# Layer 0's modulation products on four column quarters, the first norm's steps in the planned list, and new lists for both layers

## The chip, the cores and the metric

The kernel runs on one core of a Trainium2 chip. The metric is the device time of one execution in microseconds (us); before the change the median of three runs is 1832.78 us (1830.01 to 1833.64).

## What is computed

Two layers of a diffusion backbone over 512 latent tokens and 256 context tokens of width 1024, all in 32-bit floats. What matters here is the head of each layer: a conditioning vector `c` (and a second one, `c_ctx`, for the context tokens) goes through silu and is multiplied by a 1024 x 6144 matrix. The 6144 results are six vectors of 1024, which shift and scale the normalised tokens and gate the two sub-layers.

```python
mod = silu(c) @ w_mod[layer] + b_mod[layer]           # 6 vectors of 1024, for the latent tokens
mod_c = silu(c_ctx) @ w_mod[layer] + b_mod[layer]     # the same for the context tokens
sh1, sc1, g1, sh2, sc2, g2 = split(mod, 6)
h = rmsnorm(x, norm_g[0]) * (1 + sc1) + sh1           # 512 tokens; the context likewise
qa, ka, va, qr, kr, vr, gr, z, xbc, dt = split(h @ w_in[layer])
# attention, retention and a state-space group, concatenated, @ w_out, gated by g1;
# then a squared-ReLU MLP on rmsnorm(x) * (1 + sc2) + sh2, gated by g2
```

## The kernel before, in words

The 6144 columns of `w_mod` are cut into twelve sections of 512 (two for each of the six vectors). Sections 0 and 1 are the shift and 2 and 3 the scale of the first norm, 4 and 5 the first gate, 6 to 9 shift and scale of the second norm. A section is a sum over eight K-blocks of 128 rows. Layer 0's sections 0 to 9 are computed in four ways. `mod_exact` (sections 0, 2 and 3, line 370) multiplies the two-column `csil` (both conditioning vectors) in full float by one 128 x 512 block at a time, into two rows of PSUM; each product leaves two matmul records. `mod_sums` (section 1, lines 417 to 425) accumulates on VectorE and sums over the partitions with sixteen short matmul records. `mod_split` (sections 4 and 5, line 396) rounds the weights to a high part (ScalarE, line 277) and a low part (GpSimd, line 278) and multiplies both by a four-column stationary block. `mod_whole` (sections 6 to 9, line 381) is `mod_exact` with 512 KB loads of two K-blocks. `mod_cols` then turns the rows of a section into columns with four transposes (`mps`, line 208) and adds the bias.

`start` is the prologue: it loads the six token tiles (`x`), takes their norms, issues sections 0 to 3, transposes the tiles between the products (`xps`), and when all products are issued it calls `modulate` (lines 499 to 505), which scales and shifts each tile and splits it into a high part `h_h` and a low part `h_l`. One call of `modulate` is half a tile; there are twelve.

After that each layer is a set of named units (`kv0`, `xa3.`, `as20`, `md7`, ...), which are issued in the order of the written list `PLAN[layer]`. The names that matter: `kvN` the key/value projection of tile N (`kvp`, lines 523 to 525), `xwN`, `xaN`, `xbN` the state-space projection (`xbc`), `as`, `at`, `ao` scores, transposes and outputs of the attention by head, `rp`, `rs`, `rd`, `rt`, `ro`, `rn`, `ur` the steps of a retention head, `mdN` the N-th step of sections 4 to 9, a step being two K-blocks, and `woN` the first products of the output projection. The order of emission sets priorities; instructions of different units may still be exchanged on an engine by the framework's scheduler. On each engine and on the load queue of SyncE the result is one fixed order, in which an instruction that waits holds back all behind it. In layer 1 `KV_LATE` units `kv` are held behind the last matmul of layer 0's MLP.

Of the kernel before, what the change touches and what calls it, by code (L numbers as in the profile page):

```python
# [42 lines left out]
def shape_constants():  # L43
# [26 lines left out]
    KV_LATE=1,  # L70
# [5 lines left out]
    MOD="GGGVGG",  # L76
# [4 lines left out]
    CUT="443444",  # L81
)
PLAN = {
    0: """
        kv0 kv1 xw3 kv2 xa3. kv3 kv4 kv5 xa3 xb3 kp1 xw5 xa5. xa4. xa4 xc3 xb4 xc4 xt3 xa5 xb5 xc5 de xw0 kp0
        xt4 xa0. xa0 xa1. ds xb0 dr xa1 xb1 xc0 xw2 xa6. xa6 xb6 xa2. xc1 xc6 xa2 xt0 xt1 xb2 xc2 xt2 qa0. qa0
        g0 f10 f11 m1 qa1. qa1 qa2. sv00 sv01 sd01 f00 g1 f01 qa2 m0 sk b0 qa3. qa3 sd00 f20 f21 b1 sv10 si10
        qa4. qa4 sv11 si11 m2 sd11 qa5. f30 sd10 f31 qa5 sv20 m3 si20 si21 b2 zz0. sd20 sv21 sv30 zz0 sd21
        sv31 f40 f41 si30 m4 sd30 zz1. zz1 si31 zz2. zz2 sd31 f50 f51 sv41 b3 zz3. m5 zz3 si41 sd41 sv40 b4
        si40 sd40 zz4. zz4 zz5. zz5 b5 si50 si51 sg0 sg1 sg4 sg5 sg2 sg3 sn aqs rc ak0 aq0 aq1 as00 at00 as01  # L90
        at01 kr0. av as10 kr0 as02 ao00 at02 as03 at03 as04 as05 at04 at05 ao02 ao01 aq2 kr1. kr1 at10 as11
        as12 at11 kr2. kr2 ao10 kr3. kr3 at12 as13 at13 kr4. kr4 as14 kr5. ak1 ao11 aq3 as20 at20 as21 kr5
        at21 ao20 qg0. qg0 at14 as15 at15 as22 at22 as23 as24 at23 ao21 ao12 at24 as25 qg1. qg1 at25 ao22 qg2.
        qg2 aq4 as30 at30 as31 at31 ao30 qg3. qg3 as32 at32 as33 as34 at34 at33 ao31 as35 qg4. qg4 at35 ao32
        qg5. qg5 aq5 as40 at40 as41 md0 at41 ao40 as42 as43 as44 rw0 at44 at42 at43 as45 at45 ao41 md1 ao42
        as50 at50 as51 at51 md2 rl0 md3 ao50 as52 at52 as53 at53 rw1 md4 as54 at54 mx as55 rv ao51 md5 rp0
        at55 rx0 rx1 rl1 rs0 rp1 md6 rd0 md7 md8 ao52 md9 us2 md10 md11 rt0 md12 md13 md14 rd1 md15 rg0 ro00
        us0 md16 md17 md18 md19 md20 us1 ro01 ro02 md21 md22 rn0 rx2 rw2 md23 rg1 rt1 rs1 rl2 rp2 ro10 md24
        ro11 ro12 rn1 ur0 rw3 rl3 rs2 rd2 ua0 rp3 rx3 ua1 rt2 ro20 ro21 ro22 ua2 wp rg2 wo0 rs3 rn2 rd3 rg3
        rt3 wo1 wo2 wo3 ro30 wo4 wo5 ro31 ro32 rn3 wq wo6 wo7 wo8 ur1  # L100
    """.split(),
    1: """
        kv0 kv1 kv2 kv3 kv4 kv5 km0 km1 xw3 xa3. xa3 xb3 xa4. xa4 xb4 xc3 xt3 xw5 xa6. xa5. xc4 kp1 xa5 xt4 de
        xc5 xa6 kp0 xc6 xw0 xa1. ds dr xa0. xa0 xa1 xb0 xb1 xc0 xt0 xc1 xt1 xw2 xa2. xa2 xb2 xc2 xt2 qa0. g0
        f00 f10 qa0 f01 g1 m0 f11 sv00 qa1. sd00 sk qa1 m1 sv01 sd01 f20 qa2. qa2 b0 f21 sv11 sv10 b1 qa3.
        sd11 sd10 m2 zz0. f30 zz0 sv20 qa3 b2 si21 f31 m3 zz1. zz1 si20 sd20 zz2. sv21 si30 zz2 sd21 zz3. zz3
        sv30 f40 sd30 si31 aqs b3 sv31 f41 sv40 rc si40 sd31 f50 si41 sd40 m4 f51 m5 sv41 si50 sd41 b4 si51 b5
        sg0 sg3 kr0. sg1 sg2 sn aq0 av ak0 aq1 as00 at00 as01 at01 ao00 kr0 as02 at02 kr1. as03 at03 aq2 ao01
        kr1 kr2. kr2 as10 as11 at10 as12 at12 as13 at11 ao10 at13 aq3 as20 ak1 as21 at20 ao11 kr3. as22 at21
        kr3 kr4. kr4 ao20 at22 as23 at23 kr5. ao21 aq4 as30 at30 as31 as32 at31 kr5 qg0. ao30 as33 qg0 at32  # L110
        at33 ao31 qg1. qg1 aq5 as40 at40 as41 qg2. qg2 at41 as42 ao40 as50 at42 as43 qg3. at43 rw0 ao41 rv
        as51 as52 qg3 at50 at51 mx ao50 at52 as53 at53 ao51 rl0 rx0 rp0 rx1 ua0 rw1 rl1 rd0 rp1 rg1 us0 us1
        rs0 rd1 rg0 rt0 ro00 ro01 rn0 rw2 rl2 rp2 rx2 rs1 rt1 ro10 rs2 ro11 rn1 rx3 us2 ur0 rd2 rw3 rl3 rp3
        rt2 wp rd3 rg2 ro20 rs3 ro21 rn2 wo0 ua1 wo1 rg3 wo2 rt3 ro30 wo3 wo4 ua2 ro31 wo5 rn3 ur1 wq wo6 wo7
        wo8
# [18 lines left out]
def tile_hybrid_backbone(  # L134
# [166 lines left out]
    chl = cp.tile([128, KC, 4], F32R, name="chl")  # L301
    V.tensor_copy(chl[:, :, 0:4:2], csil)
    V.tensor_tensor(chl[:, :, 1:4:2], csil, chl[:, :, 0:4:2].bitcast(F32), ALU.subtract)
# [23 lines left out]
    def mod_cols(l, sec, q, nrow):  # L327
# [3 lines left out]
        if q.shape[0] == 128:  # L331
# [9 lines left out]
        if nrow == 2:  # L341
            V.tensor_tensor(tk, o, bcol, ALU.add)
        else:
            u = sm.tile([128, 4, 4], F32, tag="mc_u", name=f"mu{l}_{sec}")
            S.activation(u, o, AF.Copy)
            V.tensor_tensor(tk, u[:, :, 0:4:2], u[:, :, 1:4:2], ALU.add)
            V.tensor_tensor(tk, tk, bcol, ALU.add)
# [16 lines left out]

    def mod_exact(l, sec, raw, row):
        q = pB([2, 512], f"mq{l}_{sec}")
        for k in range(KC):
            v = raw(f"m{l}_{sec}_{k}")
            nc.sync.dma_start(v, w_mod[l, k * 128 : (k + 1) * 128, sec * 512 : (sec + 1) * 512])
            T.matmul(q, csil[:, k, :], v, start=k == 0, stop=k == KC - 1)  # L370
            yield
        r = row([2, 512], f"mr{l}_{sec}")
        S.activation(r, q, AF.Copy)
        mod_cols(l, sec, r, 2)

    def mod_whole(l, sec, row):
        q = pB([2, 512], f"mq{l}_{sec}")
        for u in range(4):
            r = wraw(wcols(w_mod[l], 0, [(sec * 512, 0, 512)])(2 * u, 2), (128, 2, 512), f"m{l}_{sec}_{u}")
            for k in range(2):  # L380
                T.matmul(q, csil[:, 2 * u + k, :], r[:, k], start=u + k == 0, stop=u + k == 4)
            if u == 3:
                r = row([2, 512], f"mr{l}_{sec}")
                S.activation(r, q, AF.Copy)
            yield
        mod_cols(l, sec, r, 2)

    def mod_split(l, sec, row):
        q = pB([4, 512], f"mq{l}_{sec}")
        for u in range(4):  # L390
            if u % 2 == 0:
                hu, lu = wunit(wcols(w_mod[l], 2 * u, [(sec * 512, 0, 512)]), (128, 4, 512), f"m{l}_{sec}_{u}", eng(KNOBS["MOD"][sec - 4]))
            h, lo = hu[:, 2 * (u % 2) : 2 * (u % 2) + 2], lu[:, 2 * (u % 2) : 2 * (u % 2) + 2]
            for k in range(2):
                for w in (h, lo):
                    T.matmul(q, chl[:, 2 * u + k, :], w[:, k, :], start=(u == 0 and k == 0 and w is h),
                             stop=(u == 3 and k == 1 and w is lo))
            if u == 3:
                r = row([4, 512], f"mr{l}_{sec}")
                S.activation(r, q, AF.Copy)  # L400
            yield
        mod_cols(l, sec, r, 4)
# [154 lines left out]
    def mixers(l, mp, hT, alloc_mix, kvw=None):  # L557
# [9 lines left out]
        par = pars[l]  # L567
# [92 lines left out]
        kv_gen = tm_group("kv", 268, [(KA, 0, 256), (DT0, 256, 12)], 6, c_kv, (pB, pC), kvw[:1])  # L660
# [7 lines left out]
        for t in range(6):  # L668
            unit(f"kv{t}", lambda t=t: kv_step(t), f"kv{t - 1}" if t else None)
# [145 lines left out]
        def conv_w(js):  # L815
            h, lo = kvw[1] if js[0] == 3 and len(kvw) > 1 else xbc_unit(l, js, eng(KNOBS["X_LO"][4 * l + {3: 0, 5: 1, 0: 2, 2: 3}[js[0]]]))
# [3 lines left out]
        for js in ((3, 4), (5, 6), (0, 1), (2,)):  # L820
            unit(f"xw{js[0]}", lambda js=js: conv_w(js))
            for j in js:
                first = {}
                unit(f"xa{j}.", lambda j=j, first=first: next(first.setdefault("g", conv_in(j, 0))), f"xw{js[0]}")
                unit(f"xa{j}", lambda first=first: next(first["g"], 0), f"xa{j}.")
                if wc or j < 5:
                    unit(f"xb{j}", lambda j=j: run(conv_in(j, 1)), f"xa{j}")
# [157 lines left out]
        for nm, n, cols, nt, consume in (("qa", 384, [(QA, 0, 384)], NQ, c_qa), ("zz", 384, [(Z0, 0, 384)], NQ, c_z),  # L985
                                         ("kr", 512, [(KR, 0, 512)], 6, c_krv), ("qg", 512, [(QR, 0, 256), (GR, 256, 256)], NQ, c_qg)):
            gen = tm_group(nm, n, cols, nt, consume, split=True)
            for t in range(nt):
                unit(f"{nm}{t}.", steps(gen), f"{nm}{t - 1}" if t else None)
                unit(f"{nm}{t}", steps(gen), f"{nm}{t}.")  # L990
# [170 lines left out]
        unit("rc", ret_const)  # L1161
# [406 lines left out]
    def start(mp, hT):  # L1568
# [3 lines left out]
        acc = mp.tile([128, 1536], F32, tag="m6", name="acc_m", bufs=KNOBS["M6"])[:, :1024].rearrange("p (s n) -> p s n", s=2)  # L1572

        def weave(a, b):
            for _ in a:
                next(b, None)
                yield
            yield from b

        row = lambda shape, name: mp.tile([128, 512], F32, tag="fcol", name=name)[: shape[0]]  # L1580

        def gens():
            yield from mod_exact(0, 0, raws[0], row)
            yield from weave(mod_exact(0, 2, raws[0], row), mod_sums(0, 1, acc, raws[1]))
            yield from mod_exact(0, 3, raws[1], row)

        gemv = gens()
# [92 lines left out]
```

## Time and profile before

| | |
|---|---|
| median of the runs | 1832.78 us |
| the profiled execution, whole | 1831.16 us |
| its span, first to last instruction | 1829.4 us |
| TensorE busy | 1737.7 us (95%) |
| VectorE busy | 1208.8 us (66%) |
| ScalarE busy | 701.7 us (38%) |
| mean granted TensorE clock | 0.979 |

Busy time of TensorE is read with care: matmuls are pipelined, so that a record is longer than the distance to the next one. Where costs are added up, the distance from start to start counts. The two stretches that the change touches most are the first 46 us, up to the first key/value product, and the stretch from 340 to 440 us, which holds the end of layer 0's attention, its retention heads and sections 4 to 9.

### The profile page before, as it was taken

To read this page: it belongs to the slowest core of one execution; us is meant where nothing else is said; L and a number is where in the kernel's file an instruction comes from. 1 tells how busy PE (TensorE), PEld (TensorE's weight loads), DVE (VectorE), ACT (ScalarE), POOL (GpSimd) and SP (SyncE) were. 2 spreads that over 40 slices of the span, in tenths; PEclk is the share of its full clock that TensorE was granted. 3 is DMA by queue.
4 is the path that set the end of the run, shared out by engine and by line. 5 is a ranking of instruction groups with operands and counts; after the bars stand their busy time and mean duration, and the time that the engine had idled before them with its cause. 6 is when DMAs were issued, how large, how long until landed. Compare 5 with 4: busy or idle time off the path is not lost. (4 is left out here: it accounts for less than half of the span.)

```text
span 1829.4 us, 24602 instructions
## 1 busy us (share of the span) xinstructions
PE 1737.7 (95%) x8991; PEld 1433.7 (78%) x8991; DVE 1208.8 (66%) x2474; ACT 701.7 (38%) x1270; POOL 342.4 (19%) x376
## 2 busy tenths in 40 slices
PE   7998999998999999999999999999988999999997
PEld 2887978657777888888888878887877788888886
DVE  5788976767567566566566587898877644444445
ACT  5553366743561201211201266545762622222222
POOL 0127222312000100100100111453121111111112
PEclk9999999998999999999999999999987999999999
DMA  8420443476435434444344443233343523333332
GB/s 282 123 61 30 133 123 101 119 204 177 162 120 137 126 105 126 128 113 117 116 116 116 128 150 116 68 106 104 106 121 85 179 67 94 102 94 100 104 95 92
DMA packets 189077, 217.00 MB, mean 119 GB/s; under 512 B 67666, under 2 KB 142236, under 8 KB 188956
## 3 DMA queue, kind: packets, MB, share of 16 engines
q1 hardware_dynamic: 188956, 215.43, 39.7%
q8 instruction: 71, 1.16, 0.3%
q14 instruction: 50, 0.41, 0.1%
HBM read 189.66 MB, written 25.72 MB: 118 GB/s over the span
## 5 line engine op out<-in xcount | busy, mean ns | idle before, releaser
L523 PE MATMUL f<-h_h,wh_f 128*128 128x512 f32 (+1 forms) x800 | 281.2, 352 | 1.4 <-ACT h_h L504 1.4
L524 PE MATMUL f<-h_l,wh_f 128*128 128x512 f32 (+1 forms) x800 | 281.7, 352 | 0.8 <-DVE h_l L505 0.8
L525 PE MATMUL f<-h_h,wl_f 128*128 128x512 f32 (+1 forms) x800 | 282.3, 353 | 0.0
L523 PE MATMUL f<-wh_g,uh 128*128 128x512 f32 x640 | 252.8, 396 | 4.6 <-DVE acc L1532 1.9
L524 PE MATMUL f<-wl_g,uh 128*128 128x512 f32 x640 | 252.5, 394 | 0.0
L525 PE MATMUL f<-wh_g,ul 128*128 128x512 f32 x640 | 251.8, 393 | 0.0
L1504 POOL TENSOR_TENSOR r<-r 128x768 f32<-128x768 f32 (+1 forms) x64 | 94.0, 1469 | 834.2 <-ACT r L1503 823.1
L277 ACT ACTIVATE wh_f<-wr_f 128x1024 fp32r<-128x1024 f32 x64 | 66.4, 1054 | 375.2 <-PE f L525 135.4
L1534 DVE TENSOR_TENSOR acc<-acc,f 128x512 f32<-128x512 f32 x140 | 96.1, 687 | 120.8 <-PE f L525 119.4
L523 PEld LDWEIGHTS f<-h_h,wh_f 128*128 128x128 f32 x800 | 153.2, 192 | 23.4 <-ACT h_h L504 1.5
L524 PEld LDWEIGHTS f<-h_l,wh_f 128*128 128x128 f32 x800 | 152.2, 190 | 23.0 <-DVE h_l L505 1.0
L525 PEld LDWEIGHTS f<-h_h,wl_f 128*128 128x128 f32 x800 | 152.4, 191 | 20.9
L461 DVE SCALAR_TENSOR_TENSOR ga<-wr_mg,cg_a,ga 128x512 f32<-128x512 f32 x216 | 153.7, 764 | 15.2 <-DMA wr_mg<-in_w_mod_dram 15.1
L523 PEld LDWEIGHTS f<-wh_g,uh 128*128 128x128 f32 x640 | 120.1, 188 | 33.9 <-DVE acc L1532 2.3
L525 PEld LDWEIGHTS f<-wh_g,ul 128*128 128x128 f32 x640 | 120.2, 188 | 28.6
L524 PEld LDWEIGHTS f<-wl_g,uh 128*128 128x128 f32 x640 | 120.3, 188 | 27.3
L1503 ACT ACTIVATE r<-f 128x768 f32<-128x768 f32 (+1 forms) x64 | 44.7, 698 | 192.2 <-PE f L525 128.2
L1505 DVE CAST uh<-r 128x768 fp32r<-128x768 f32 (+1 forms) x64 | 32.3, 505 | 123.7 <-POOL r L1504 123.7
L278 DVE TENSOR_TENSOR wl_g<-wr_g,wh_g 128x1024 fp32r<-128x1024 f32 x62 | 76.7, 1242 | 53.8 <-ACT wh_g L277 53.8
L278 DVE TENSOR_TENSOR wl_f<-wr_f,wh_f 128x1024 fp32r<-128x1024 f32 x64 | 77.7, 1221 | 50.1 <-ACT wh_f L277 50.1
L277 ACT ACTIVATE wh_g<-wr_g 128x1024 fp32r<-128x1024 f32 x64 | 67.3, 1056 | 96.6 <-DMA wr_g<-in_w_ff_dram 55.2
L523 PE MATMUL xbc<-h_h,wh_xbc 128*128 128x512 f32 (+1 forms) x208 | 71.9, 345 | 1.9 <-ACT cin L785 1.9
(403 smaller groups left out, 3711.0 us busy)
## 6 DMA issues: line engine op xcount, KB each, us to landing
wr_f<-in_w_ff_dram SPq DMA_DIRECT2D x64, 512.0 KB, 3.8
wr_g<-in_w_ff_dram SPq DMA_DIRECT2D x64, 512.0 KB, 3.6
wr_mg<-in_w_mod_dram SPq DMA_DIRECT2D x192, 128.0 KB, 2.9
wr_m<-in_w_mod_dram SPq DMA_DIRECT2D x24, 512.0 KB, 4.0
m<-in_w_mod_dram SPq DMA_DIRECT2D x32, 256.0 KB, 5.1
wr_o<-in_w_out_dram SPq DMA_DIRECT2D x16, 512.0 KB, 4.2
wr_xbc<-in_w_in_dram SPq DMA_DIRECT2D x14, 512.0 KB, 5.4
xmid<-xt SPq DMA_DIRECT2D x10, 512.0 KB
```

The lines of the kernel that those rows point to most:

```text
L277: S.activation(hv[:, a0 : a0 + an], r, AF.Copy)
L278: (lo_eng or V).tensor_tensor(lv[:, a0 : a0 + an], r, hv[:, a0 : a0 + an].bitcast(F32), ALU.subtract)
L461: V.scalar_tensor_tensor(acc[:, s], r2[:, k % 2], w, acc[:, s], ALU.mult, ALU.add)
L523: T.matmul(o, a[0], b[0], start=first, stop=False)
L524: T.matmul(o, a[0], b[1], start=False, stop=False)
L525: return T.matmul(o, a[1], b[0], start=False, stop=last)
L1503: S.activation(r, q[:, :NT], AF.Relu)
L1504: G.tensor_tensor(r, r, r, ALU.mult)
L1505: V.tensor_copy(uh, r)
L1534: V.tensor_tensor(acc[tt][:, ns], acc[tt][:, ns], qs[tt][half], ALU.add)
```

## The change

The products of layer 0's ten sections all take one form. The stationary block is `cwide[:, k, :]`, `csil` widened from 2 to 32 columns with zeros, and K-block k goes to rows 32j to 32j+31 of a 128 x 512 PSUM tile, j = k mod 4. Each quarter thus sums two K-blocks. The four transposes of `mod_cols` become four products of the 128 x 512 copy with `qsum`, a 128 x 2 matrix that adds the four quarters and turns rows into columns at once. `mod_split` is gone, with its conversions, and section 1 no longer uses VectorE.

The prologue is cut into units (`xl` load, `xq` square, `xr` root, `xs` scale, `xu` transpose, `xm` modulate by half tile, `mo` one K-block of sections 0 to 3, `kw`, `pc`, `pr` loads of weights and parameters), and `kv` into halves of four K-blocks; these stand in the list with the rest. Both lists are written anew, and `KV_LATE` goes from 1 to 4.

```diff
-    chl = cp.tile([128, KC, 4], F32R, name="chl")
+    cwide = cp.tile([128, KC, 32], F32, name="cwide")
+    G.memset(cwide, 0.0)
+    G.tensor_copy(cwide[:, :, 0:2], csil)
+    qsum = cp.tile([128, 2], F32, name="qsum")
+    V.tensor_reduce(qsum, ident.rearrange("p (j r) -> p r j", r=32)[:, 0:2, :], AX.X, ALU.add)
...
             for k in range(4):
-                transpose(o[:, k, :], q[:, k * 128 : (k + 1) * 128])
+                T.matmul(o[:, k, :], q[:, k * 128 : (k + 1) * 128], qsum, start=True, stop=True)
...
+    def mod_quarter(q, k, v):
+        j = k % 4
+        T.matmul(q[32 * j : 32 * j + 32], cwide[:, k, :], v, start=k < 4, stop=k >= KC - 4)
...
     def mod_exact(l, sec, raw, row):
-        q = pB([2, 512], f"mq{l}_{sec}")
+        q = pB([128, 512], f"mq{l}_{sec}")
...
-            T.matmul(q, csil[:, k, :], v, start=k == 0, stop=k == KC - 1)
+            mod_quarter(q, k, v)
...
-                yield from (mod_whole if sec >= 6 else mod_split)(0, sec, row)
+                yield from mod_whole(0, sec, row)
...
-    KV_LATE=1,
+    KV_LATE=4,
...
 PLAN = {
     0: """
-        kv0 kv1 xw3 kv2 xa3. kv3 kv4 kv5 xa3 xb3 kp1 xw5 xa5. xa4. xa4 xc3 xb4 xc4 xt3 xa5 xb5 xc5 de xw0 kp0
...
+        xl0 xl2 xl3 xl4 xl5 xq0 xl1 xq4 xq3 xq1 xq2 xq5 xr0 xs3 mo00 xs0 xs4 mo01 mo02 xs2 pc mo03 xs5 mo04
+        mo05 mo06 xs1 mo10 mo20 mo21 mo22 xu2 mo07 xu3 xu1 xu0 mo08 mo23 mo11 mo12 mo13 xu5 mo24 mo14 mo25
+        mo15 mo26 mo27 mo16 mo17 mo28 mo18 kw xm02 mo30 mo31 xu4 mo32 mo33 mo34 mo35 mo36 mo37 mo38 xm10 xm11
+        xm01 xm00 xm03 xm12 xm05 xm15 pr kv0. xm13 kv0 kv1. xm04 kv1 kv2. kv2 xw3 xa3. kv3. xm14 kv3 kv4. kv4
...
-        us0 md16 md17 md18 md19 md20 us1 ro01 ro02 md21 md22 rn0 rx2 rw2 md23 rg1 rt1 rs1 rl2 rp2 ro10 md24
+        md7 md8 ao52 rd0 md9 us2 md10 md11 rt0 md12 md13 rg0 md14 rd1 md15 ro00 us0 md16 md17 rx2 md18 md19
```

## Rows read from the trace of the kernel before

**Rows 1.** The page's first part: busy us, share of the span, instructions.
```profile
PE 1737.7 (95%) x8991; PEld 1433.7 (78%) x8991; DVE 1208.8 (66%) x2474; ACT 701.7 (38%) x1270; POOL 342.4 (19%) x376
```
**Rows 2.** Windows of the prologue: busy us of engines, clock, DMA share, GB/s.
```profile
core 0: us, PE busy (x) PEld busy (x) DVE busy (x) ACT busy (x) POOL busy (x), PEclk, DMA share, GB/s
10.00:20.00 10.00, 6.81 (x12) 1.15 (x13) 2.05 (x13) 7.26 (x10) 0.00 (x0) 1.00 0.86 285
30.00:40.00 10.00, 10.00 (x55) 5.33 (x55) 8.90 (x18) 4.37 (x9) 0.00 (x0) 1.00 1.05 331
50.00:60.00 10.00, 9.87 (x78) 9.54 (x77) 7.99 (x21) 10.00 (x23) 0.00 (x0) 1.00 0.30 97
```
**Rows 3.** Timeline of TensorE in the prologue: start, us, operation, count [idle before].
```profile
13.19 3.57 PE L370 MATMUL mq<-m,csil 128*2 128x512 f32 x4 [9.60 <-DMA m<-in_w_mod_dram]
26.48 1.88 PE L370 MATMUL mq<-m,csil 128*2 128x512 f32 x4
28.29 1.10 PE L208 MATMUL xps<-ident,x 128*128 128x128 f32 x8
29.31 1.02 PE L370 MATMUL mq<-m,csil 128*2 128x512 f32 x2
36.73 1.84 PE L425 MATMUL mq<-sel,acc_m 128*128 128x1 f32 x16
38.50 7.03 PE L370 MATMUL mq<-m,csil 128*2 128x512 f32 x16
48.55 0.41 PE L208 MATMUL mps<-ident,mr 2*128 2x2 f32 x4 [1.96 <-ACT mr L373]
```
**Rows 4.** Timeline of the load queue: the last three weight loads of section 3.
```profile
36.56 0.33 SPq L369 DMA_DIRECT2D m<-in_w_mod_dram  x1
...
39.55 0.33 SPq L369 DMA_DIRECT2D m<-in_w_mod_dram  x1
...
40.41 0.33 SPq L369 DMA_DIRECT2D m<-in_w_mod_dram  x1
```
**Rows 5.** All products of the sections, by line: min/median/max ns, first and last start.
```profile
L381 PE MATMUL mq<-wr_m,csil x64: 591/592/593, 356.7 to 418.0; 128*2 128x512 f32 x64
L396 PE MATMUL mq<-wh_m,chl x16: 387/396/397, 341.9 to 360.1; 128*4 128x512 f32 x16
L396 PE MATMUL mq<-wl_m,chl x16: 387/394/472, 342.1 to 360.3; 128*4 128x512 f32 x16
L277 ACT ACTIVATE wh_m<-wr_m x8: 1042/1060/1081, 284.0 to 354.2; 128x1024 fp32r<-128x1024 f32 x8
L278 POOL TENSOR_TENSOR wl_m<-wr_m,wh_m x8: 2374/2392/2706, 285.1 to 355.3; 128x1024 fp32r<-128x1024 f32 x8
```
**Rows 6.** Timeline of TensorE in the stretch of sections 4 to 9.
```profile
341.85 0.39 PE L396 MATMUL mq<-wh_m,chl 128*4 128x512 f32 x1
342.08 0.39 PE L396 MATMUL mq<-wl_m,chl 128*4 128x512 f32 x1
...
370.08 1.02 PE L381 MATMUL mq<-wr_m,csil 128*2 128x512 f32 x2
...
394.07 0.41 PE L208 MATMUL mps<-ident,mr 4*128 4x4 f32 x4
394.40 1.88 PE L381 MATMUL mq<-wr_m,csil 128*2 128x512 f32 x4
...
413.25 5.31 PE L381 MATMUL mq<-wr_m,csil 128*2 128x512 f32 x12
```
**Rows 7.** Windows of that stretch, and of the half clock in it.
```profile
340.00:380.00 40.00, 38.18 (x204) 21.98 (x202) 30.19 (x65) 30.95 (x63) 15.62 (x8) 1.00 0.65 177
380.00:440.00 60.00, 54.02 (x275) 33.37 (x276) 38.80 (x113) 17.01 (x32) 8.94 (x11) 0.89 0.77 215
...
420.00:440.00 20.00, 15.51 (x87) 14.70 (x87) 14.10 (x37) 6.32 (x11) 6.61 (x7) 0.66 0.83 213
```
**Rows 8.** TensorE's longest wait in that stretch, in the timeline.
```profile
432.53 1.51 PE L208 MATMUL sT<-ident,ry 128*128 128x128 f32 x6 [3.27 <-DVE ry L1269]
```
**Rows 9.** TensorE's two waits where layer 1 begins, in the timeline.
```profile
1094.21 1.09 PE L208 MATMUL nps<-ident,tt 128*128 128x128 f32 x8 [3.88 <-ACT tt L510]
...
1103.73 0.39 PE L525 MATMUL kvp<-wh_kv,h_l 128*128 128x268 f32 x1 [1.91 <-POOL h_l L505]
```

More of the change, by code (lines that the diff above doesn't have):

```diff
@@ L81 @@
     CUT="443444",
+    SECS="EEEE",
+    RAW="0101",
 )
@@ L90 @@
[L90 to L94, printed above, removed]
@@ L116 @@
+        wo5 rn3 ur1 wq wo6 wo7 wo8
     """.split(),
@@ L330, in mod_cols @@
         k0 = 4 * (sec % 2)
-        if q.shape[0] == 128:
+        if len(q.shape) == 3:
             o = q
@@ L386, in mod_whole @@
         mod_cols(l, sec, r, 2)
[L388 to L402, printed above, removed]
     def mod_sums(l, sec, acc, raw=None):
@@ L1566, in load_par, with start @@
             nc.sync.dma_start(pars[l][:, o : o + n], ap.partition_broadcast(128))
[L1568 removed]
+    def start(mp, hT, kvw, unit):
         raws = [lambda name, tag=tag, n=n: mp.tile([128, 776], F32, tag=tag, name=name, bufs=n)[:, :512]
                 for tag, n in (("u3", 6), ("t3", KNOBS["T3"]))]
[L1572 to L1578, printed above, removed]
[L1580 to L1591 removed]
@@ new lines, in start, with mod_step @@
+        row = lambda shape, name: mp.tile([128, 512], F32, tag="fcol", name=name)[: shape[0]]
+        gens = {}
+        def mod_step(sec):
+            if sec not in gens:
+                raw = raws[int(KNOBS["RAW"][sec])]
+                if KNOBS["SECS"][sec] == "S":
+                    acc = mp.tile([128, 1536], F32, tag="m6", name=f"acc_m{sec}", bufs=KNOBS["M6"])[:, :1024]
+                    gens[sec] = mod_sums(0, sec, acc.rearrange("p (s n) -> p s n", s=2), raw)
+                else:
+                    gens[sec] = mod_exact(0, sec, raw, row)
+            return next(gens[sec], 0)
@@ new lines, in mod_end @@
+        def mod_end(sec):
+            while mod_step(sec) != 0:
+                pass
+        unit("pc", lambda: load_pcol(0))
+        unit("pr", lambda: load_par(0))
+        unit("kw", lambda: kvw.append(kv_unit(0)))
+        for sec in range(4):
+            for k in range(KC):
+                unit(f"mo{sec}{k}", lambda sec=sec: mod_step(sec), f"mo{sec}{k - 1}" if k else None)
+            unit(f"mo{sec}8", lambda sec=sec: mod_end(sec), f"mo{sec}7", "pc")
+        xT = {}
+        big9, big6 = [], []
@@ new lines, in start @@
+        groups = ((0, 6),)
+        for t0, t1 in groups:
+            unit(f"xr{t0}", lambda t0=t0, t1=t1: x_root(t0, t1), *[f"xq{t}" for t in range(t0, t1)])
+        for tt in range(6):
+            unit(f"xl{tt}", lambda tt=tt: x_load(tt), f"xl{tt - 1}" if tt in (1, 3) else None)
+            unit(f"xq{tt}", lambda tt=tt: x_square(tt), f"xl{tt}")
+            unit(f"xs{tt}", lambda tt=tt: x_scale(tt), f"xr0")
+            unit(f"xu{tt}", lambda tt=tt: x_turn(tt), f"xs{tt}")
+            for h in range(2):
+                unit(f"xm{h}{tt}", lambda tt=tt, h=h: x_mod(tt, h), f"xu{tt}", f"mo{h}8", f"mo{2 + h}8")
```

153 lines of the change are left out of this document (75 added, 78 removed).

## The prediction, made before the changed kernel was built

> **What bounds the kernel now.** I read the page's first part, then the windows and TensorE's timeline of the two stretches that the change touches, then TensorE's waits there. The page says TensorE: busy 95% of the span, with VectorE at 66% and ScalarE at 38% [rows 1]. So TensorE's work and its few waits set the time, and an edit is worth what it takes from TensorE's line, or from a wait in it.
>
> In the prologue two things are close together. The DMA engines are full (share 1.05, 331 GB/s from 30 to 40 us) and TensorE is busy through the same window, while from 10 to 20 us the loads reach only 285 GB/s [rows 2]. Section 3's sixteen records run back to back from 38.50, at (7.03 - 0.59)/15 = 0.43 us each [rows 3, 5]; they do not wait for their data. The last two loads are issued at 39.55 and 40.41, against 36.56 for the one before [rows 4], because the buffers are still being read. So the end of section 3, at 38.50 + 7.03 - about 0.1 = 45.4 us, is TensorE's, with the loads a few us ahead of it. Behind it TensorE stands 1.96 us for the copy of that section [rows 3].
>
> From 340 to 440 us TensorE is busy 92 of 100 us [rows 7]. It has one long wait, 3.27 us at 432.53, for retention's VectorE steps [rows 8], and the granted clock averages 0.66 from 420 to 440 [rows 7], a mixture of its levels 1.2 and 2.4 GHz. All products of the sections are over at 418.6 [rows 5], so they fill nothing there.
>
> **Cost of one K-block.** Now, in full float: two records at 0.43 = 0.86 us [rows 3]. In `mod_split`: two at 342.08 - 341.85 = 0.23, so 0.46 [rows 6]. The new form has no row. Its ends are: no overlap, 0.86; and all four quarters beside each other, 0.86/4 = 0.215. I take a value between them: the two records of one product share a quarter and should follow each other, but the first record of the next product, on another quarter, may run beside the second of this one. A run of n adjacent K-blocks then takes n + 1 steps of 0.43: 0.86 alone, 1.29 for two, 4.73 for ten. I keep both ends for the range.
>
> No row shows two matmuls of a kind on different quarters. The Trainium skill (TensorE: Matmul & The Clock Gate, Part 3, Packing small matmuls) says that column tiles do run beside each other, 2.38 times faster with three of them, while matmuls start and end in program order. By that figure a K-block would take about 0.86/2.38 = 0.36 us in a dense run, and sections 4 to 9 would gain some 11 us more than in the sum below, by estimate. Nothing in the trace of before can confirm it.
>
> **Part 1, the prologue.** TensorE gets section 1's eight K-blocks and loses its sixteen short records (1.84 us [rows 3]); VectorE loses 14 accumulations. Four sections are 32 K-blocks; in the new list most stand next to each other, some on the same quarter, so I count 38 steps, 16.3 us. With 48 transposes at (1.10 - 0.28)/7 = 0.12 [rows 3], 5.6 us, and four `qsum` steps it is about 27 us from 13.2 us on, plus the slower first records (3.57 us for four) and changes of shape: about 42.5. A `qsum` step is eight records of the kind of section 1's, (1.84 - 0.25)/15 = 0.106 us apart [rows 3], so 0.85 us against 0.33 for four transposes [rows 6]. The loads would allow about the same end: without the wait for buffers the last two go out at about 37.4 and 38, so 2.4 to 3 us earlier than in [rows 4]. Section 3 then ends near 42.5 instead of 45.4: **-3 us**. Behind it ScalarE is full for 10 of 10 us [rows 2], with the twelve half tiles. The list puts the half tiles that need only sections 0 and 2 among the products, and halves of `kv` can run on them; this can hide the 1.96 us or put the same wait elsewhere. Ends for the part: -6 and +1 with overlap.
>
> **Part 2, sections 4 to 9.** Before: 32 x 0.23 + 64 x 0.43 + 6 x 0.33 = 7.4 + 27.5 + 2.0 = 36.9 us of TensorE [rows 5, 6]. After: sections 6 to 9 stand in runs of up to five units; 32 K-blocks in about nine runs are 41 steps, 17.6 us. Sections 4 and 5 lie among attention, in lone units: 16 K-blocks are 10.3 us when the two of a unit stay together, 13.8 when they are parted, as nearly all are at 356 to 384 us (pairs of records like the one at 370.08 [rows 6]). Six `qsum` steps are 5.1. Together 33.0 to 36.5: -3.9 to -0.4, of which I take **-3 us**. TensorE is nearly full there, so this reaches the end; what is late next is retention's chain on VectorE (38.8 of 60 us busy [rows 7]). With four quarters at once it would be 10.3 + 5.1 = 15.4, -21.5 on TensorE, of which the chains would let through perhaps half; without overlap 41.3 + 5.1, +9.5, of which some 3 us would fall into the waits.
>
> `mod_split`'s conversions go: eight of 1.06 us on ScalarE and eight of 2.39 us on GpSimd [rows 5]. ScalarE is busy 31 of 40 us from 340 to 380 [rows 7] and TensorE rarely waits for it, so **-1 us**. The copy of 128 x 512 in place of 2 x 512 has the same length of rows and costs nothing more on ScalarE. The loads stay 512 KB a unit; `cwide` and `qsum` are three small instructions before the first product, hidden behind the 9.60 us wait for data [rows 3], and would cost their own few tenths if that were gone.
>
> **Part 3, the lists.** Most of layer 0's order and layer 1's stays. `KV_LATE` holds three more units behind the last MLP product; what queues behind them is TensorE's own later work. The trace has 3.88 and 1.91 us of waits there [rows 9], on norm steps of ScalarE and GpSimd; a new order can remove them or double them. Ends -5 and +5, value **-1 us**.
>
> **Sum.** -3 - 3 - 1 - 1 = -8 on the profiled execution's 1831.16 gives 1823; the median of the runs is 1.6 us higher, so **1823 to 1825**, and I take 1823.5.
>
> **Rivals.** *No overlap*, the slower side: a K-block costs 0.86 everywhere. The prologue, where TensorE has no slack from 24 us on, gains 6.9 - 1.8 + 4 x 0.85 - 3 x 0.33 = 7.5 us of work; sections 4 to 9 gain 9.5, less 3 in the waits; -2 for the rest: +12, 1843. For it: no row shows overlap. Against: the products write four separate row ranges. It decides from 0.66 us a K-block on, where 48 x 0.66 + 5.1 = 36.9.
>
> *Each change of shape empties the array.* Products now sit among full-width matmuls at little cost: four records, then transposes, take 28.29 - 26.48 = 1.81 against 4 x 0.43 = 1.72 [rows 3]. If every entry and exit cost a record's tail, 0.59 - 0.43 = 0.16 us, some 24 lone groups in sections 4 to 9 and eight in the prologue would pay 32 x 2 x 0.16 = 10 us, and the gain is gone: about 1833. The Trainium skill (TensorEngine Tiling (Array Packing), Key Properties) states that changing the tiling mode drains the engine, which speaks against this change; the row of 0.09 us tells only of narrow blocks as they are now.
>
> *Four quarters at once*: part 1 -5, part 2 -11, the rest -2: 1813.
>
> *Products as padding*: if they only fill waits, less of them leaves new waits and more of the low clock seen at 420 to 440; part 2 is 0 and the sum -5, 1826, inside the forecast.
>
> **How the numbers follow.** Partial overlap, 1816 to 1828: 0.48 (the padding case is in it). Four at once, 1806 to 1816: 0.16. Emptying, 1828 to 1837: 0.17. No overlap, 1837 to 1850: 0.14. A new list that costs more than it brings, 1837 and above: 0.05. The bound of what can be told from no change is 0.2%, 3.7 us. Faster: the first two and a little of the third, 0.65; same, most of the third, 0.14; slower 0.21. The range leaves out about one in ten at each end: 1809 to 1841.
>
> **What would show it.** Distances between product records: 0.43 from one K-block to the next in a run if the forecast holds, 0.86 without overlap, 0.2 with four at once. The first key/value product near 42 us instead of 45.5. The last section near 410 instead of 418. No wait of TensorE over 2 us between 42 and 60 us. I am wrong above all if K-blocks are not issued next to each other, or if the new lists move the waits of the long middle, which I have costed at almost nothing.

## The result, and the profile after

The changed kernel takes 1856.95 us (median of four runs, 1854.89 to 1858.28) against 1833.02 for the kernel before (four runs on the same chip, 1830.01 to 1833.64): a ratio of 1.0129, 95% interval 1.0099 to 1.0159. It is 24 us slower, where 1823.5 was forecast, and above the range's upper end of 1841. In the page's first part TensorE is hardly busier than in [rows 1], while the span is 23.7 us longer; VectorE, ScalarE and GpSimd have less to do.

```profile
PE 1749.0 (94%) x9035; PEld 1453.8 (78%) x9035; DVE 1194.6 (64%) x2455; ACT 696.4 (38%) x1261; POOL 314.7 (17%) x370
```

The time is lost in two places. Layer 0's last key/value product starts at 76.64 us instead of 69.05, and the shift is +8.0 at the last `qgp` product (348.3 against 340.3). The last output-projection product starts at 547.1 instead of 521.4, +25.7. Behind that some 2 us are won back (1853.1 against 1829.4 at the end, +23.7). The lines are, for the kernel before and the changed one, the last `kvp`, `qgp` and `op` products of layer 0:

```profile
69.05 0.28 PE L525 MATMUL kvp<-wh_kv,h_l 128*128 128x268 f32 x1
76.64 0.28 PE L517 MATMUL kvp<-wh_kv,h_l 128*128 128x268 f32 x1
340.26 0.40 PE L525 MATMUL qgp<-wh_qg,h_l 128*128 128x512 f32 x1
348.26 0.39 PE L517 MATMUL qgp<-wh_qg,h_l 128*128 128x512 f32 x1
521.38 0.39 PE L525 MATMUL op<-wh_o,mix_l 128*128 128x512 f32 x1
547.06 0.40 PE L517 MATMUL op<-wh_o,mix_l 128*128 128x512 f32 x1
```

The windows of the changed kernel (columns as in [rows 2]) answer to [rows 2, 7]:

```profile
10.00:20.00 10.00, 4.92 (x12) 1.10 (x13) 2.04 (x14) 5.69 (x11) 0.00 (x0) 1.00 0.94 336
30.00:40.00 10.00, 9.36 (x53) 4.17 (x51) 3.01 (x6) 2.90 (x5) 0.00 (x0) 1.00 0.90 263
40.00:50.00 10.00, 5.55 (x28) 2.73 (x28) 7.74 (x22) 8.31 (x19) 0.28 (x6) 0.71 0.56 180
50.00:60.00 10.00, 8.97 (x46) 6.00 (x47) 4.56 (x14) 4.94 (x12) 0.42 (x1) 0.78 0.51 158
340.00:380.00 40.00, 37.33 (x208) 22.92 (x207) 24.96 (x60) 24.39 (x55) 1.47 (x1) 1.00 0.58 176
380.00:440.00 60.00, 52.76 (x269) 35.61 (x270) 28.95 (x90) 16.21 (x34) 6.08 (x9) 0.74 0.60 169
420.00:440.00 20.00, 17.47 (x62) 10.87 (x63) 4.91 (x17) 1.31 (x3) 1.93 (x4) 0.58 0.71 194
460.00:480.00 20.00, 19.43 (x80) 16.88 (x79) 14.13 (x30) 8.29 (x10) 6.36 (x4) 0.64 0.33 93
```

The reader is to look at the third number from the right, the granted clock. It was 1.00 before 60 us and 0.89 from 380 to 440 in the kernel before [rows 2, 7]; now it is 0.71 and 0.78 in the prologue's end, 0.74 from 380 to 440, and still 0.64 at 460 to 480. The loads reach 263 GB/s from 30 to 40 us, 331 before.

TensorE's timeline in the prologue shows both the size of a K-block and the new waits:

```profile
15.09 3.21 PE L371 MATMUL mq<-m,cwide 128*32 128x512 f32 x6 [11.56 <-DMA m<-in_w_mod_dram]
...
31.46 1.90 PE L371 MATMUL mq<-m,cwide 128*32 128x512 f32 x10
33.30 1.09 PE L213 MATMUL xps<-ident,x 128*128 128x128 f32 x8
34.32 1.91 PE L371 MATMUL mq<-m,cwide 128*32 128x512 f32 x6
...
43.86 1.72 PE L371 MATMUL mq<-m,cwide 128*32 128x512 f32 x8
48.81 0.59 PE L515 MATMUL kvp<-wh_kv,h_h 128*128 128x268 f32 x1 [3.23 <-ACT h_h L496]
...
50.83 1.92 PE L371 MATMUL mq<-m,cwide 128*32 128x512 f32 x4
...
56.51 1.05 PE L345 MATMUL mps<-qsum,mr 128*128 128x2 f32 x8 [0.72 <-ACT mr L381]
57.43 0.37 PE L515 MATMUL kvp<-wh_kv,h_h 128*128 128x268 f32 x1
```

Of the ten records at 31.46 the first eight are four K-blocks: their first records start at 31.462, 31.469, 31.475 and 31.489, their second ones at 31.915 to 31.942, and the fifth K-block at 32.345. So four quarters run at once, and a K-block is 0.883/4 = 0.22 us in such a run. The first product starts at 15.09 us, 1.9 us later than in [rows 3], because its weights land later. The last record of section 3 starts only at 55.2, behind the first key/value products, where [rows 3] had all sixteen records done by 45.5.

In the stage of sections 4 to 9 the same work stands at both clock levels:

```profile
354.98 1.05 PE L371 MATMUL mq<-wr_m,cwide 128*32 128x512 f32 x4 [0.78 <-DMA wr_m<-in_w_mod_dram]
...
407.41 1.52 PE L1226 MATMUL rd<-vrr,W 128*128 128x64 f32 x12 [1.06 <-DVE rst L1241]
...
427.38 1.92 PE L371 MATMUL mq<-wr_m,cwide 128*32 128x512 f32 x4
...
450.26 1.47 PE L213 MATMUL sT<-ident,ry 128*128 128x128 f32 x6 [5.12 <-DVE ry L1272]
...
468.72 2.82 PE L1226 MATMUL rd<-vrr,W 128*128 128x64 f32 x12
471.30 0.77 PE L515 MATMUL op<-wh_o,mix_h 128*128 128x512 f32 x1
```

Two K-blocks take 1.05 us at 2.4 GHz and 1.92 at 1.2 GHz; twelve `rd` records 1.52 and 2.82. So a microsecond at half clock, if TensorE is busy in it, gives away 1 - 1.05/1.92 = 0.45 to 1 - 1.52/2.82 = 0.46. The output projection began at 439.03 in the kernel before, so this point has moved by 32.3 us. The wait of [rows 8] has grown from 3.27 to 5.12.

### The profile page after: what moved, and what is told of

It is laid out like the page before. It is cut to its first block, busy times and chain, and to the rows that moved or that the text cites. A ratio compares the mean times of both kernels' runs of the same rounds, so it can differ in the third digit from the quotient of the medians.

```text
span 1853.1 us, 24663 instructions
## 1 busy us (share of the span) xinstructions
PE 1749.0 (94%) x9035; PEld 1453.8 (78%) x9035; DVE 1194.6 (64%) x2455; ACT 696.4 (38%) x1261; POOL 314.7 (17%) x370
## 5 line engine op out<-in xcount | busy, mean ns | idle before, releaser
L283 DVE TENSOR_TENSOR wl_g<-wr_g,wh_g 128x1024 fp32r<-128x1024 f32 x62 | 76.6, 1241 | 49.7 <-ACT wh_g L282 49.7
```

Of the source, the lines that this page charges most:

```text
L283: (lo_eng or V).tensor_tensor(lv[:, a0 : a0 + an], r, hv[:, a0 : a0 + an].bitcast(F32), ALU.subtract)
```

## The experiments

*Form* stands for the 32-column stationary block on the quarters with `qsum`, *lists* for the new lists and the prologue's units. Clock is the mean granted clock, averaged over a kernel's runs (0.976 for the kernel before, 0.961 for the changed one). The ratio is taken to runs of the kernel before from the same round; the median of these moves between rounds from 1832.7 to 1834.3, so a difference of two medians from different rounds is uncertain by 1 to 2 us. Views are of one execution of each kernel, which can lie off the median: e1's took 1855.5 us, e2's 1848.6, e11's 1836.9 (the shortest of ten) and e13's 1845.7 (the longest of twelve).

| run | median us | ratio to before, 95% interval | clock |
|---|---|---|---|
| e1 form but sections 4, 5, old lists | 1845.2 | 1.0074 [1.0045, 1.0103] | 0.963 |
| e2 form, old lists | 1840.1 | 1.0044 [1.0021, 1.0066] | 0.966 |
| e3 two-column products, new lists | 1848.7 | 1.0087 [1.0064, 1.0111] | 0.972 |
| e4 changed, layer 1's old list | 1855.4 | 1.0128 [1.0099, 1.0157] | 0.962 |
| e5 e2, products twice | 1858.7 | 1.0127 [1.0097, 1.0157] | 0.970 |
| e6 changed, products twice | 1865.9 | 1.0179 [1.0156, 1.0202] | 0.969 |
| e7 e3's prologue, old list behind | 1841.5 | 1.0040 [1.0026, 1.0054] | 0.977 |
| e8 old prologue, new list behind, old forms | 1837.7 | 1.0026 [1.0004, 1.0048] | 0.976 |
| e9 e2, prologue's order pinned | 1839.8 | 1.0037 [1.0015, 1.0058] | 0.964 |
| e10 before, filling | 1836.4 | 1.0017 [0.9997, 1.0037] | 0.980 |
| e11 changed, filling | 1842.5 | 1.0056 [1.0034, 1.0078] | 0.973 |
| e12 changed, prologue's order pinned | 1856.1 | 1.0110 [1.0075, 1.0145] | 0.960 |
| e13 e9, filling in layer 0 | 1840.1 | 1.0030 [1.0009, 1.0052] | 0.969 |
| e14 e13, twice as much filling | 1834.8 | 1.0005 [0.9990, 1.0020] | 0.974 |
| e15 e13, groups of four K-blocks as written | 1841.6 | 1.0041 [1.0020, 1.0062] | 0.969 |
| e16 e12, filling in layer 0 | 1851.6 | 1.0103 [1.0069, 1.0137] | 0.966 |
| e17 e9, new list behind the prologue | 1844.9 | 1.0053 [1.0033, 1.0073] | 0.964 |
| e18 form in the prologue alone, pinned | 1828.4 | 0.9969 [0.9953, 0.9985] | 0.974 |

### Form and lists apart: e1 to e4

e1 and e2 put the form into the kernel before and leave both lists; e2 moves sections 4 and 5 over too:

```diff
-                yield from (mod_whole if sec >= 6 else mod_split)(0, sec, row)
+                yield from mod_whole(0, sec, row)
```

> The kernel before, with its lists and prologue, and the products of sections 0, 2, 3 and 6 to 9 on four quarters with the qsum step; section 1 stays on VectorE, 4 and 5 stay split. Theory A (the new order is what costs: products stand on TensorE where they hold their buffers, and the load queue behind them): the form itself is harmless, so 1820 to 1834 us. Theory B (the form is what costs: cheap products leave TensorE idle between waits, and the clock falls): 1840 us or more, with a granted clock under 0.70 somewhere between 380 and 450 us.

> As the first one, and sections 4 and 5 also whole on quarters, without the conversions. Theory A: 1815 to 1832 us, a little below the first. Theory B: 1842 to 1855 us, above the first, since still less TensorE work is left between the waits.

e3 is the changed kernel with the old products and transposes; in e4 only layer 1's list and `KV_LATE` go back.

```diff
-        q = pB([128, 512], f"mq{l}_{sec}")
+        q = pB([2, 512], f"mq{l}_{sec}")
...
-            mod_quarter(q, k, v)
+            T.matmul(q, csil[:, k, :], v, start=k == 0, stop=k == KC - 1)
```

> The changed kernel with its new lists, but all ten sections in the two-column form with transposes: the order alone. TensorE's work grows by 80 K-blocks times 0.86 - 0.22 us = 51 us at most against the changed kernel. Theory A: 1860 us or more, since the order costs and the products cost more as well. Theory B: at or below 1845 us, since the products keep TensorE and its clock busy.

> The changed kernel with layer 1's old list and KV_LATE 1 (the halves of kv next to each other). The two traces stand 24 us apart where layer 1 begins and 24 us apart at the end, so both theories expect 1857 us, within 5; a time under 1850 would put part of the loss into layer 1.

e1 came out where theory B had put it; e2 and e3 lie between the two theories (1840.1 against 1832 and 1842, 1848.7 against 1860 and 1845). Both parts cost by themselves: the form +7 to +12 us, e3 +16, and together +24. e3's +16 isn't all order: its sections 1, 4 and 5 are two-column products too, by the prediction's costs 5 + 16 x (0.86 - 0.46) = 11 us of work more than in the kernel before. From e3 to the changed kernel TensorE loses work and the time rises by 8. Layer 1's list and `KV_LATE` do nothing (e4 within 1.5 us of the changed kernel, with overlapping runs). The clock falls mostly with the form: to 0.963 to 0.966 with the form alone, to 0.972 in e3.

### Putting work back: e5 and e6

```diff
-        T.matmul(q[32 * j : 32 * j + 32], cwide[:, k, :], v, start=k < 4, stop=k >= KC - 4)
+        for i in range(2):
+            T.matmul(q[32 * j : 32 * j + 32], cwide[:, k, :], v, start=k < 4 and i == 0, stop=k >= KC - 4 and i == 1)
```

with half of each weight in `cwide`.

> The quarters with the old lists (the run before with all of sections 4 to 9 on quarters), with every product issued twice at half the weight: the same loads, order, buffers and waits, and TensorE's product work doubled. Theory B (the cheap form leaves TensorE idle in sections 4 to 9 and the granted clock falls there, which makes everything behind it longer): with the work put back the clock stays high, half-clock time between 340 and 480 us falls from about 50 us to about 20, and the time falls to about 1833, the kernel before, though TensorE has more to do. Theory A (what the form costs is its place in the order, its loads or its sums): the time stays at 1840 or rises by the 10 us of added products.

> The changed kernel with every product issued twice at half the weight. Theory B: the clock's part goes and the lists' part stays, so about the time of the new lists with two-column products, 1847 to 1850, with half-clock time between 340 and 480 us falling from 55 us to about 35. Theory A: 1857 or more, since TensorE has more to do and nothing else is changed.

Both times went up, by 18.5 and 9, so theory B's numbers were missed: e6 lies where theory A had put it (1857 or more), e5 above both. Theory B's sign on the clock held (0.966 to 0.970, 0.961 to 0.969). The repair was badly sized: a second copy in a lone group costs another 0.9 us, so that sections 4 to 9 take 51.7 us of TensorE in e5, start to start, against 36.3 in e2 and 41.4 in the kernel before.

### Where the lists cost: e7 and e8

e7 takes e3's list up to the first key/value step and the old one behind it; e8 has the old prologue and the new list behind it, with sections 4 and 5 split as before. Their diffs are the lists'.

> Two-column products and transposes, with the first norm as units in the new order up to the first key/value step, and behind that the old list of layer 0 and of layer 1. If the lists' cost is that of the prologue and of the later part, added up: about 1838 (+6, all of it before 60 us, and none in sections 4 to 9). If all of the lists' +16 comes from the later part: 1833. If the delay in the prologue itself brings the later loss with it: 1845 and above.

> The kernel before with its own prologue and two-column products, and the new list of layer 0 from the first key/value step on, with key/value steps in halves; sections 4 and 5 on their split products. If the later part of the list costs by its order: about 1843 (+10), with the loss between 380 and 480 us and more half-clock time there. If it costs only together with the prologue or the changed sections 4 and 5: 1833 to 1836.

e7 came out at +8, with a last key/value product 6.5 us late and a clock as before; e8 at +4, less than the +10 expected and hardly clear of no change, so the two don't add up to e3's +16. Part of e7's loss is no order at all: the units put section 1 on TensorE, and with two-column products that is 8 x 0.86 - 1.84 = 5 us of work [rows 3]. e3, with sections 4 and 5 in two columns as well, and e7 thus overstate the new list's own cost.

### The prologue's order: e9 and e12

The prologue's list is not the order that TensorE runs. In e2, whose list is the old one, the timeline has transposes ahead of the third product of section 0, waiting for ScalarE:

```profile
16.29 0.47 PE L208 MATMUL pps<-ident,prow 125*128 125x125 f32 x1
17.93 1.54 PE L208 MATMUL xps<-ident,x 128*128 128x128 f32 x6 [1.17 <-ACT x L1619]
19.41 1.92 PE L380 MATMUL mq<-m,cwide 128*32 128x512 f32 x2
```

In the kernel before, section 0's eight products stand ahead of the first transpose. The scheduler has exchanged them. A product that stands late holds its buffer, and the load queue waits for it, which is the row of the queue's waits from 12 to 50 us in the kernel before, in e2 and in the changed kernel:

```profile
SPq L369 <- PE mq L370: 3.7, 5, 1.7
```
```profile
SPq L386 <- PE mq L380: 10.0, 7, 4.5
```
```profile
SPq L377 <- PE mq L371: 12.6, 8, 2.6
```

(us in total, times, longest.) The edit holds the order of emission:

```diff
+                with tc.issue_after(last_mq[0].ins):
+                    for k in range(KC):
+                        transpose(q[:, k, :], xT[tt][:, k * 128 : (k + 1) * 128])
```

and the same for layer 0's key/value products.

> The quarters with the old lists (the run with all of sections 4 to 9 on quarters), and TensorE's order in the prologue held to that of the kernel before: a tile's transposes stay behind the product that was emitted ahead of them, and the key/value products behind section 3's last one. Theory C (in the prologue the cost is the scheduler's exchange: transposes and key/value products that wait for ScalarE and VectorE moved ahead of products whose buffers the next loads need): the last key/value product of layer 0 comes at 66 to 69 us instead of 73.9, SyncE's waits for product buffers fall from 10 to about 4 us, and the time falls by some 5 us to about 1835. Rival (the prologue is bound by the loads, or by the granted clock after a thin stretch): the last key/value product stays at 73 or later and the time at 1840.

> The changed kernel with the same two pins: transposes behind the product ahead of them in its list, key/value products behind section 3's last one. Theory C: last key/value product at about 69 instead of 76.6, time about 1849. Rival (the new list's own order, in which the first half tiles and the loads come late): no gain, or a later last key/value product, 1857 or more.

In e9 the order's part in the late prologue is shown, and the median does not follow. The queue's wait falls, though not to the 3.7 of the kernel before, and the last key/value product starts at 69.28, 0.2 us behind that of the kernel before:

```profile
SPq L391 <- PE mq L385: 6.8, 6, 2.7
```

Yet the median stays at 1839.8. In its profiled execution the lead is there until 340 us (-0.3 against the kernel before, +4.4 in e2), and is given back from there to the end of the output projection, +18. In the changed kernel (e12) the pins bring the last key/value product from 76.6 to 74.3, and the median by 0.8 where 8 was forecast; the queue still waits:

```profile
SPq L382 <- PE mq L376: 10.5, 9, 2.5
```

So most of what is late there is not the scheduler's exchange but the new prologue's own order and section 1's products in it; which of the two was not told apart. The loss of the form is in the stage of sections 4 to 9.

### Filling: e10 and e11

Matmuls that compute nothing, written into tiles that the real ones then overwrite:

```diff
+    def filler(o, n):
+        for _ in range(2 * n):
+            T.matmul(o[:, 0:256], ident.bitcast(BF16)[:, 0:128], ident.bitcast(BF16), start=True, stop=True)
...
             q = pA([128, TOK], f"sT{l}{kc}")
+            filler(q[:, 0:512], 3)
```

and one such call each in front of the scores (1) and the outputs (2) of a retention head.

> The kernel before, with matmuls that compute nothing in layer 0's and layer 1's retention: 54 of 128 x 256 in bf16 a layer, in front of the transposes to the mix, of the scores and of the outputs, written into the tiles that the real ones overwrite. Theory B (the clock falls where TensorE has little in these stages, and a microsecond at half clock costs about half of one): half-clock time from 340 to 480 and from 1340 to 1430 falls from 44 us to under 15, a gain of some 15 us against at most 13 us for the added records where no wait hides them: 1823 to 1833. Rival (the clock goes by something that such filling does not change): half-clock time as before, and 1840 to 1846 by the added work.

> The changed kernel with the same filling. Theory B: half-clock time from 340 to 490 us falls from 55 us to under 25 and with it the time to 1840 to 1850. Rival: half-clock time as in the changed kernel, and 1862 to 1870.

Adding 108 matmuls to the changed kernel made it 14.4 us *faster*, within the forecast and with the two ratios' intervals apart, with the clock from 0.961 to 0.973. The windows from 340 to 490 us of the kernel before, the changed kernel and e11:

```profile
340.00:490.00 150.00, 140.47 (x728) 94.55 (x727) 103.35 (x264) 72.64 (x140) 32.29 (x24) 0.95 0.64 184
```
```profile
340.00:490.00 150.00, 133.15 (x679) 95.31 (x678) 88.22 (x229) 57.08 (x109) 19.39 (x18) 0.82 0.55 163
```
```profile
340.00:490.00 150.00, 136.71 (x792) 97.99 (x791) 94.98 (x246) 62.85 (x124) 19.65 (x18) 0.93 0.60 181
```

A mean of 0.82 between the levels 1 and 0.5 is 2 x 0.18 x 150 = 54 us at half clock; 0.95 is about 15 and 0.93 about 21. In the changed kernel TensorE does *less* from 340 to 490 than before, in records and in busy time, and is slower at it; with the filling it does more and gets further. The same filling cost the kernel before 3.5 us (1823 to 1833 was forecast), with an interval that reaches no change: it had little half clock to win back there, and its clock still rose, from 0.976 to 0.980. That the granted clock carries the changed kernel's loss in this stage is shown by e11 as far as one edit can: from the last `qgp` to the last output-projection product e11 takes 185.6 us, the changed kernel 198.8. The filling also changes what the scheduler exchanges.

### Form and lists at a held clock: e13 to e16

e13 and e16 have the pins, and the filling in layer 0 alone; e14 has about twice the filling; e15 writes the products of sections 4 to 9 in groups of four K-blocks:

```diff
-            for k in range(2):
-                mod_quarter(q, 2 * u + k, r[:, k])
+            pend.append(r)
+            if u % 2:
+                for k in range(4):
+                    mod_quarter(q, 2 * (u - 1) + k, pend[-2 + k // 2][:, k % 2])
```

> Quarters with the old lists and the prologue's order pinned, and the filling of 54 matmuls in layer 0's retention alone. Theory B with the sizes measured so far (the filling took some 44 us of half clock from the changed kernel, at 0.48 us each, and costs about 5 us a layer): 1840 - 21 + 5, so 1824, under the kernel before, with a mean granted clock of 0.975 in place of 0.964. Rival (the form with the old lists is slow in sections 4 to 9 for another reason, a chain that the filling only delays): 1840 to 1845.

> The same with more filling in layer 0: 112 matmuls, in front of retention's sums too. Theory B: less half clock than with 54, at most 20 us more of it gained (10 us of time), against some 6 us more work: between 4 us faster and 6 us slower than with 54. Rival (filling is only work): 6 us slower than with 54, and clock as there.

> The kernel with 54 fillings, and sections 4 to 9 in groups of four K-blocks: a step of an even number only loads, the next one issues the products of both. The group of two costs about 0.9 us now, four beside each other about 0.9 too, so 12 groups and 10.8 us of TensorE's time go. If that time is worth what it is at full clock: 1824 - 10.8 + the loads' waits, so 1814 to 1820. If thinner products only lower the clock again (theory B to its end): within 3 us of the kernel with 54 fillings.

> The changed kernel with its prologue's order pinned and 54 fillings in layer 0. Theory B: 1856 - 21 + 5, so 1840. What it then stays above the same with the old lists (1824) is what the new lists cost by their order at a like clock, some 10 to 16 us. Rival: 1856 or more.

e13 is a miss: the clock rose half as far as expected (0.964 to 0.969) and paid for the filling, no more. In the profiled executions the stage from the last `qgp` to the last output-projection product did go from 199.4 us (e9) to 190.5; behind that stage this execution, the longest of e13's, loses 9 us again, with 17 us more at half clock. e14 answers it: with more to do again the time falls by 5 us to that of the kernel before, and the clock to 0.974; the two ratios' intervals still overlap a little.

e15 is no test of its question. The 96 product records of its sections 4 to 9 stand on TensorE in 18 groups of the same sizes as e13's, and take as long (the records of `mq` alone, e13 and e15):

```profile
335.00:490.00 155.00, 25.73 (x96) 3.64 (x96) 0.00 (x0) 3.58 (x6) 0.88 0.60 175
335.00:490.00 155.00, 25.31 (x96) 3.60 (x96) 0.00 (x0) 3.58 (x6) 0.90 0.61 182
```

The 10.8 us that were to go did not go, so that its time within 1.5 us of e13 says nothing of theory B.

e16 missed its 1840. It stands 11.5 us over e13, and the intervals are apart. Of this some 5 us go with its clock, 0.966 against 0.969 (13 us more at half clock, at 0.36 to 0.46 each); the 6 to 9 left are what the new lists cost, with section 1's products, which stand on TensorE in e16 alone. In the profiled executions it is in the prologue: the last key/value product starts at 78.2 us in e16 and 71.3 in e13, and the stage of sections 4 to 9 is no longer in e16. The windows of e13 and e14 have 0.87 and 0.91:

```profile
340.00:490.00 150.00, 137.19 (x760) 100.04 (x759) 91.83 (x241) 60.41 (x115) 19.44 (x18) 0.87 0.61 178
```
```profile
340.00:490.00 150.00, 139.43 (x812) 101.31 (x812) 90.45 (x241) 60.11 (x114) 19.05 (x18) 0.91 0.61 178
```

### Stage by stage: e17 and e18

e17 is e9 with the new list of layer 0 behind the old prologue. e18 is e9 with sections 4 to 9 in their old forms:

```diff
-                yield from mod_whole(0, sec, row)
+                yield from (mod_whole if sec >= 6 else mod_split)(0, sec, row)
...
-        q = pB([128, 512], f"mq{l}_{sec}")
+        q = pB([2, 512], f"mq{l}_{sec}")
```

> The kernel before's prologue with quarters and its order pinned, sections 4 to 9 on quarters, and behind the prologue the new list of layer 0 (key/value steps in halves). Parts the new list's prologue from its rest. If the lists' cost at a like clock (some 7 to 11 us between the two filled kernels) is all in the prologue's units: 1838 to 1842, as with the old list. If the later part of the new list costs with quarters as it did with two-column products (+4): 1843 to 1846. If it brings the whole of it: 1850 and more.

> Quarters for sections 0, 2 and 3 alone, pinned order, old lists, and sections 4 to 9 as in the kernel before. If all of the form's loss lies in sections 4 to 9, as the marks of the pinned kernel say (+0.2 us at the last key/value product, +18 us behind the output projection): 1831 to 1835, half-clock time from 340 to 480 us below 25 us. If a thin prologue alone sets the later stages back: 1838 or more.

The later part of the new list costs 5 us by the medians (e17 against e9), but 3 by the ratios, whose intervals overlap: it is not shown. e18 beats both kernels, and its forecast of 1831 to 1835: 1828.4 us, 0.9969 of the kernel before (0.9953 to 0.9985). Putting sections 4 to 9 back takes 11.5 us from e9 (12.5 by the ratios), and the windows of e9 and e18 say how:

```profile
340.00:490.00 150.00, 138.56 (x666) 102.57 (x665) 84.94 (x224) 56.28 (x103) 18.24 (x18) 0.74 0.59 172
```
```profile
340.00:490.00 150.00, 141.10 (x737) 94.96 (x736) 104.10 (x267) 74.23 (x142) 32.96 (x24) 0.97 0.65 184
```

78 us at half clock with quarters, 9 without. Where e18's 5 to 6 us against the kernel before come from is not settled: in the two profiled executions its last output-projection product is 1.1 us earlier and the stretch from there to layer 1's first key/value product, the same instructions, 5.5 us shorter.

## Why the prediction was wrong, point by point

**What bounds the kernel.** Right as to TensorE, wrong as to what an edit is worth: it said "an edit is worth what it takes from TensorE's line, or from a wait in it". From 340 us on the rate of that line was itself a result of the edit: 41 us more at half clock (54.6 against 13.7 between 340 and 490), which the sum had put at nothing.

**The K-block.** The size was wrong in the favourable direction. Two adjacent K-blocks were put at 1.29 us; at 354.98 the next instruction starts 0.98 us behind them. Four at once, the low end, is what the chip does. By the page's figure for three column tiles (the Trainium skill, TensorE: Matmul & The Clock Gate, Part 3, Packing small matmuls) a K-block was estimated at 0.36 us in a dense run; the trace has 0.22, and the measurement decides. But in sections 4 to 9 fourteen of the nineteen groups on TensorE hold one or two K-blocks, and these cost 0.9 to 1.0 us, as four would. That the wide copy costs ScalarE nothing more was nearly right: 597 ns, against 570 for two rows. *Four quarters at once* was right about the chip and, at 1813, 44 us off in time.

**Part 1, -3 us.** It became +7.6 at the last key/value product. The step that failed is "without the wait for buffers the last two go out at about 37.4 and 38": the last load of section 3 went out at 46.03, because products now stand late in TensorE's order and hold their buffers, 12.6 us of waits for them against 3.7:

```profile
45.57 0.80 SPq L377 DMA_DIRECT2D m<-in_w_mod_dram  x2
```

I counted work, and read the list as the order. With the old list, holding the order (e9) lets the prologue end as before; with the new one (e12) it wins back 2.3 of the 7.6 us, so the list as written holds its buffers too, and its first product is 1.9 us late. There was also a slip in the sum: 16.3, 5.6 and four `qsum` steps of 0.85 make 25.3, not 27. The `qsum` step was sized right (0.85 forecast, 31.46 - 30.58 = 0.88 measured).

**Part 2, -3 us.** The stage from the last `qgp` to the last output-projection product went from 181.1 to 198.8 us. Summed from start to start, with the waits between them, sections 4 to 9 take 34.5 us of products and 7.7 of `qsum`, against 41.4 before, so it looks as if nothing were won. But 15 of these 42.2 were spent at half clock. The whole stage can be taken apart by the trace's records of TensorE and of its clock: idle time rose from 9.5 to 16.9 us, busy time at half clock from 11.1 to 53.4, and all busy time, counted at full clock with 0.455 given away per us at half, fell from 166.6 to 157.6. So the work came out even better than forecast, and the loss is -9.0 + 7.4 + 0.455 x 42.3 = 17.6. That this closes is no proof, as the work is what is left over. The test is that kernels with the same instructions in this stage come out at the same work at different clocks: 154.4 in e2 and 154.5 in e9, with 52.8 and 73.5 us at half clock, and 166.6 and 166.2 in the kernel before and e18; the filling of layer 0 adds 6.5 to the kernel before (e10) and 6.7 to e9 (e13). In e9 the account is -12 + 2 + 28 = 18. Over whole kernels and averages of runs, e9 less e18 is +11.5 to +12.5 us with a clock of 0.964 against 0.974, which is 38 us more at half clock. At the 0.36 us each that 135 runs of the 18 kernels show (each kernel's own mean taken off) that is 14, at 0.46 each 17: at a like clock sections 4 to 9 on quarters gain some 1 to 6 us by this estimate, and the -3 is not refuted.

**The rival that came true** is *products as padding*. It named "new waits and more of the low clock seen at 420 to 440" and priced them at nothing: "part 2 is 0 and the sum -5". The low clock and the waits came as it said, and part 2 was not 0 but +18. That the products did nothing but fill waits was wrong: 9 us of work did go. [rows 7] held a hint of the price: 20 us at a clock of 0.66, some 14 us at half clock, where no products stand any more [rows 5]. How much further this would reach no row said.

**Part 3, -1 us.** "Most of layer 0's order and layer 1's stays" was the failed step, as to the prologue: the new lists with section 1's products cost 6 to 9 us at a like clock (e16 against e13), and what the part behind the prologue costs is not clear of noise (e17 against e9). Layer 1's list is worth nothing (e4), within the bounds of -5 and +5. *A new list that costs more* was given 0.05, and is a part of what happened.

**ScalarE, -1 us**, was not told apart by any run; e1 to e2 (-5 us, with overlapping intervals) holds it together with the new form of two sections. *Emptying* is not seen: eight transposes and the quarter products behind them at 34.32 start 1.02 us apart, as did those ahead of the two-column products at 29.31 in [rows 3]. *No overlap* is refuted by the first records.

**The signs.** Those of the forecast did not come: the distance in a run of four is 0.22, the sign of *four at once*; the first key/value product came at 48.81 instead of 42, behind a wait of 3.23 us, and the last product of the sections starts at 440.6 instead of near 410.

**The chances.** 0.21 for slower took in only cases in which the form or the list was expensive by itself. The case in which it is cheap and the stage behind it pays was put inside the forecast.

## What to carry to other kernels

Taking work off the busiest engine is worth its time only if the engine's rate stays: before an edit, read the granted clock beside the busy time of each stretch, and price the stretch at both levels when the edit removes the dense work that stands in it. Where a framework's scheduler may exchange instructions, a cheaper instruction also changes the order; look at the order on the engine, and at who waits for the buffers of what moved. An order written in the source need not be the one that runs: e15's edit left the groups as they were. Try a faster form stretch by stretch: here sections 0, 2 and 3 alone, with their order held, came out 5 to 6 us under the kernel before, and the whole change 24 over it.

## What the runs showed of the chip that was not expected

Four products of 32 columns on four row ranges of one PSUM tile take the time of one: 0.88 us from the first start to the next K-block's, against 8 x 0.43 for the old form. Records of one full-float product are parted for it: all first records stand ahead of all second ones.

TensorE can be busy for 17.47 of 20 us (420 to 440) and be granted 0.58 of its clock. In that stretch it did short full-float records of 64 columns with groups of two K-blocks between them; the clock came back behind the first output-projection products at 471.30. Why groups of quarters do not hold it, where runs of two-column products do, is open: doubling the products (e5) took back about half of the added time at half clock (54.6 us in e2, 34.1 in e5, 13.7 in the kernel before).

Within one kernel the time differs between runs by up to 21 us (e1, 1836.8 to 1858.0), and follows the mean granted clock of the run, 0.968 and 0.956 at these two ends.
